# A 128-byte pad behind the bias table, and another start for the weights of the seven-product tiles: the phase in SBUF of matmul operands in a one-core decoder layer

## The chip, the core and the metric

One Trainium2 chip, of which the kernel uses one core. The metric is device time in microseconds, the median of three runs; lower is better. Matmuls run on TensorE (PE, with its weight loads listed as PEld), elementwise work on VectorE (DVE), ScalarE (ACT) and GpSimd (POOL); SyncE (SP) issues the transfers. SBUF is the on-chip memory: 128 partitions, and in each of them tiles lie one behind another. The *phase* of an operand is here its byte address within a partition, modulo 256.

## The reference

A decoder layer for 512 tokens of width 1024 in float32: a SwiGLU FFN of width 2816, a mixer of three parallel branches (sparse attention, gated delta rule, cross-attention into 256 memory tokens), and a second FFN.

```python
h = swiglu(rms_norm(x, ffn1_pre_norm[l]), ffn1_w_gate[l], ffn1_w_up[l], ffn1_w_down[l])
x = x + 0.5 * rms_norm(h, ffn1_post_norm[l])
u = rms_norm(x, mix_pre_norm[l])
nsa_q, nsa_kv, nsa_g, dn_qkv, dn_a, dn_b, dn_z, mem_q = split_cols(u @ w_in[l], IN_SPLITS)
...
gates = jax.nn.sigmoid(u @ w_branch_gate[l]).reshape(b, s, N_BRANCH, d)
merged = (gates[:, :, 0] * (o_nsa @ w_branch_nsa[l])
          + gates[:, :, 1] * (o_dn @ w_branch_dn[l])
          + gates[:, :, 2] * (o_mem @ w_branch_mem[l]))
x = x + rms_norm(merged @ w_out[l], mix_post_norm[l])
h = swiglu(rms_norm(x, ffn2_pre_norm[l]), ffn2_w_gate[l], ffn2_w_up[l], ffn2_w_down[l])
x = x + 0.5 * rms_norm(h, ffn2_post_norm[l])
```

## The kernel before

**Split products.** A float32 product is made of three products of rounded operands (type float32r): each operand is a high part, rounded, and a low part, the rest; `mm3` (lines 117 to 119) adds high by high, low by high and high by low in one PSUM bank. Weights come in pieces of 128x512 (256 KB): `wload` (line 105 the transfer into `wraw`, line 106 the rounding into `whi` on ScalarE, line 109 the rest `wlo` on VectorE). Tokens lie in `xth` and `xtl`, eight pieces of 128x512 each.

**Which operand is moving.** A matmul loads 128 columns of one operand (the stationary one) and streams the other (the moving one). In `prod_fm` the weights are stationary and `xth`/`xtl` move: gate and up products, projections, merge gates. In `tm_prod` and `down_half` the tokens or hidden parts (`Hh`, `Hl`) are stationary and the weights move; the down product of FFN 2 rounds most of its weights into a ring (`ringr`, `ringh`) that lies where `xth` and `xtl` did.

**Seven-product tiles.** From the seventh tile on, both FFNs make gate and up by a scheme of seven products in place of eight (`fast_load`, `fast_tile`): per tile 7 x 4 x 3 = 84 matmuls of 256 columns at line 429. The transformed tokens lie in `thi` and in low parts `txa`, `txb`, `tmth`, `tmtl`. The weights of even and odd tiles alternate between two sets: one in a tile `fset` (high, and behind it low parts), one in the room of `xth` and `xtl`, by then free (`fxth`, `fxtl`). `fast_set` lets a set begin `OFFW` floats behind the start of its room.

**Where things lie.** The pools stand one behind another. In the first one (`cp`) come the constants (4096 bytes per partition, from a multiple of 256 on), `xth`, `xtl` (16384 each), `RB` (1024), the room with the tag `mth` and that with the tag `mtl`. A room is as large as its largest tile. For `mth` this is the bias table's one-hot operand, 4 x 504 + 128 floats, 8576 bytes, which is 33.5 times 256; so `mtl` and every pool behind it begin at a phase of 128. In the built program the operands of the large groups have these phases:

| group (line) | moving | stationary |
|---|---|---|
| gate, up, projections: `xth`/`xtl` by `whi`/`wlo` (117 to 119) | 0 | 128 |
| `w_vs`, `w_z`: `whi`/`wlo` by `xth`/`xtl` | 128 | 0 |
| down product: `whi`/`wlo` by `Hh`/`Hl`; `w_out` | 128 | 128 |
| down product of FFN 2, ring: `ringh` (`wlo`) by `Hh`/`Hl` | 0 (128) | 128 |
| seven products, `fset`: `thi`, `txa`, `txb`, `tmtl` (`tmth`) | 128 (0) | 64 |
| seven products, `fxth`: the same | 128 (0) | 192 |
| attention logits `KH`/`KL` by `qa` (1039) | 128 | 128 |

**The start.** The first 256 tokens come in two halves of columns, the other 256 (`xb`) later. A list (`order_s` in `PRM`) says in which order pieces of work are written: `w` a weight load of the first two tiles, `P` half of their products, `t` a transposition of two column blocks with its rounding (lines 198 to 201), `x` the load of the later tokens, `n` their squares, inverse root and scaling (lines 184, 129 to 139, 187, 188), `R` the row scale `RB` of the first tokens (lines 229 to 238), `F` the gate of a tile for a half of the tokens (with its products, where `P` did not make them; lines 300 to 306), `B` the loads of the bias table, `c` those of the other constants. `offs` raises the priority of a piece by a number of places in the scheduler. Each engine takes its instructions strictly in the order so found, and SP its transfers.

Of the kernel before, what the change touches and what calls it, by code (L numbers as in the profile page):

```python
# [10 lines left out]
F32 = mybir.dt.float32  # L11
# [6 lines left out]
P = 128  # L18
# [7 lines left out]
NH = 8  # L26
# [4 lines left out]

C_ID, C_TRI, C_NEG, C_LVL, C_EYE, C_END = 0, 128, 256, 384, 768, 1024
M_BM, M_HB = 0, 8
PAD = 88


PRM = {'order': ['i', 'a', 'w', 'c01', 'h01', 'r0', 'c00', 'c10', 'c02', 'l0', 'h00', 'h02', 'c12', 'k0', 'h10', 'c11', 'c22', 'h12', 'h11', 'h22', 'r1', 'k1', 'l1', 'c21', 'h21', 'b0', 'e0', 'z', 'c20', 'r2', 'h20', 'c32', 'k2', 'l2', 'c31', 'd00', 'h31', 'r3', 'd01', 'l3', 'b1', 'd02', 'x0', 's00', 'e1', 'd10', 'c30', 'h32', 'x1', 'd11', 's01', 'h30', 's02', 's03', 'q3', 'p0', 'd12', 'o0', 'p1', 'q0', 'p2', 'p3', 'k3', 's10', 'p4', 'q1', 'p5', 's11', 'p6', 'p7', 's12', 's13', 'o1', 'q2', 'f'], 'dma': {'l': 'sync', 'b': 'sync', 'd': 'scalar', 'c': 'sync', 'r': 'sync'}, 'off': {'b0': 300, 'h31': 400, 'r1': 50, 'h32': 50, 'h11': 100, 'h12': 200, 'd10': 100, 'A01': 100, 'A10': 100, 'A11': 100, 'A20': 400, 'A31': 100, 'A21': 20, 'x0': 20, 'x1': 20, 'L': 200, 'S310': 400, 'S001': 20, 'S311': 400, 'A30': 100, 'r0': 400, 'd02': 20, 's11': 100, 'V20': 400, 'l3': 100, 'q1': 20, 'f': 400, 'l1': 50, 'h20': 100, 'h22': 100, 'r3': 50, 'P010': 50, 'y': 100, 'h02': 50, 'S101': 20, 'A00': 100, 'Q0': 50, 'Q1': 200, 'Q2': 50, 'Q3': 50, 'P110': 400, 'V31': 400, 'd01': 200, 'o0': 400, 'p0': 50, 'p1': 400, 'p2': 400, 'p4': 400, 'p5': 400, 'p6': 400, 'p7': 400, 'b1': 200, 'h01': 100, 'M15': 20, 'P201': 400, 'e0': 100, 'e1': 100, 'o1': 20, 'q0': 50, 'q2': 20, 'h21': 20, 'd11': 50, 'p3': 400, 'U0': 100, 's13': 50, 'c11': 20, 's00': 200, 'P011': 400, 'M14': 200, 'c20': 50, 'k2': 20, 'M03': 20, 'V00': 400, 'V01': 400, 'V10': 400, 'V11': 400, 'V21': 400, 'V30': 400, 'l2': 200, 'h00': 400, 'G0': 20, 'S210': 20, 'P101': 200, 'i': 100, 'G2': 20}, 'ph': 'e', 'po': 'ss', 'xpd': (0, 1, 2), 'order2': ['K1', 'K0', 'B', 'M10', 'Q0', 'C0', 'Q1', 'S000', 'S001', 'P000', 'C3', 'P001', 'C1', 'S010', 'P010', 'C2', 'S011', 'V00', 'Q2', 'S101', 'S100', 'P011', 'S110', 'V01', 'M12', 'P100', 'W0', 'P101', 'S111', 'Q3', 'P110', 'S200', 'S210', 'V10', 'P111', 'V11', 'P200', 'M14', 'M15', 'S201', 'P201', 'S211', 'W1', 'V20', 'P211', 'P210', 'V21', 'S301', 'W2', 'S300', 'S311', 'M11', 'P300', 'P301', 'L', 'M13', 'S310', 'G0', 'V30', 'M16', 'G2', 'P311', 'M17', 'P310', 'V31', 'W3', 'A00', 'M00', 'A01', 'G1', 'U0', 'M05', 'A10', 'A11', 'G3', 'A30', 'A31', 'U3', 'U1', 'M03', 'M06', 'A20', 'A21', 'U2', 'M07', 'M22', 'M20', 'M02', 'M24', 'M27', 'M21', 'M23', 'M01', 'M25', 'M04', 'M26'], 'order0': ['d0', 'p0', 'n0', 't0', 'd1', 'k2', 'k0', 'p2', 'p3', 'v', 'k3', 'n1', 'k1', 't1'], 'order3': ['s2', 's3', 's7', 's6', 's5', 's1', 's0', 's4', 'd00', 'd01', 'd11', 'g', 'p0', 'd10', 'n0', 't0', 'p1', 'n1'], 't3': (('mm', 'r'), ('e', 's')), 'pool': {'W2': 2, 's13': 3, 'k0': 0, 'k1': 0, 'k2': 0, 'k3': 2, 'p3': 1, 'C0': 1, 'C1': 0, 'C2': 0, 'C3': 2, 'S310': 0, 'L': 3, 'd11': 3, 'p0': 1, 'p1': 1, 'p2': 1, 'p4': 2, 'p5': 1, 'p6': 1, 'p7': 1, 'S311': 0, 'h01': 0, 'h00': 2, 'h02': 0, 'h10': 0, 'h11': 0, 'h12': 0, 'h22': 0, 'h21': 0, 'h20': 0, 'h31': 0, 'h30': 3, 'h32': 0, 'i': 2, 'P011': 2, 'c21': 0, 'd01': 2, 'S000': 0, 'S001': 0, 'S010': 0, 'S011': 0, 'S100': 0, 'S101': 0, 'S110': 0, 'S111': 0, 'S200': 0, 'S201': 0, 'S210': 0, 'S211': 0, 'S300': 0, 'S301': 0, 'M24': 2, 'G2': 2, 'A01': 0, 'M10': 0, 'M15': 2, 'M12': 2, 'M14': 2, 'M13': 2, 'M17': 2, 'M11': 2, 'M16': 2, 'M23': 0, 'M27': 3, 'M01': 2, 'M00': 2, 'M03': 0, 'M07': 2, 'M06': 1, 'M22': 2, 'M04': 2, 'M20': 2, 'M26': 2, 'M02': 0, 'M21': 2, 'M25': 2, 'M05': 2, 'c11': 1, 'o1': 3, 'P000': 2, 'P001': 1, 'P010': 2, 'P100': 2, 'P101': 2, 'P110': 2, 'P111': 2, 'P200': 2, 'P201': 2, 'P210': 2, 'P211': 2, 'P301': 0, 'P300': 3, 'P310': 2, 'P311': 2, 'c12': 3, 'b1': 1, 'x0': 0, 'x1': 0, 'V21': 0, 'c30': 0, 'c01': 0, 'c02': 0, 'c00': 0, 'c10': 0, 'c22': 0, 'c20': 0, 'c31': 0, 'c32': 0, 's01': 3, 'A31': 0, 'd12': 0, 'y': 2, 'G0': 2, 'G1': 2, 'G3': 0, 'U3': 0, 'W3': 2, 'r1': 2, 's12': 3, 'U2': 0, 'Q0': 2, 'Q1': 2, 'Q2': 2, 'Q3': 1, 's00': 3, 's02': 2, 's03': 3, 's10': 2, 's11': 3, 'e1': 2, 'd00': 1, 'U0': 0, 'U1': 0, 'l2': 0, 'd02': 2, 'K1': 3, 'V11': 0, 'V00': 2, 'r2': 0, 'l3': 3}, 'pool3': {'d00': 3, 'd01': 3, 'd10': 3, 'd11': 0, 'p1': 2, 't1': 3, 't0': 3, 's5': 2, 's7': 2, 's1': 2, 's0': 2, 's3': 2, 's6': 2, 's2': 2, 's4': 2, 'q0': 1}, 'pool0': {}, 'off0': {'p3': 20, 'n1': 50, 'k2': 400, 'k1': 20, 'p2': 100, 'p0': 400}, 'off3': {'s1': 20, 's5': 200, 'g': 200, 't0': 200, 'd10': 200, 'p0': 200, 'n0': 200}, 'tt': ('e', 's'), 'order_s': ['t00', 'w010', 'w000', 't01', 'P00', 'w110', 'y', 'w100', 'P10', 't02', 'w011', 'w001', 't03', 'P01', 'w111', 'w101', 'R0', 'F000', 'P11', 'x', 'n', 't10', 'F200', 't11', 'F101', 't12', 't13', 'F110', 'B', 'F211', 'F011', 'c'], 't0': ('e', 's'), 'rs': ((0, 0), (0, 0)), 'ra': (1, 1), 'warm': 8, 'pools': {'F000': 0, 'F101': 0, 'F200': 0, 'F011': 0, 'F110': 0, 'F211': 0, 'w10': 0, 'w11': 1, 't00': 0, 't01': 0, 't02': 0, 't03': 0, 't13': 0, 't10': 0, 't11': 0, 't12': 0, 'w00': 0, 'w01': 0, 'w000': 0, 'P01': 0}, 'ptc': 'vvs', 'cva': 'v', 'offs': {'t13': 100, 'R1': 400, 't03': 20, 't02': 20, 'w001': 100}, 'vnc': 's', 'sp3': 0, 'hsc': 'vv', 'sf2': 2, 'psc': 'vvvv', 'sp1': 0, 'vbs': 'v', 't1c': 'vs', 'sgv': 256}


class Body:  # L40
    def __init__(self, ctx, tc, a, out, tap):
        self.tc, self.nc, self.a, self.out, self.tap = tc, tc.nc, a, out, tap
        pool = lambda name, **k: ctx.enter_context(tc.tile_pool(name=name, **k))
# [267 lines left out]

    OFFW = 48
    T_B11, T_B21, T_B22, T_T1, T_T2, T_T3, T_T4 = range(7)
    S_A11, S_A12, S_A22, S_S3, S_S1, S_S4, S_S2 = range(7)

# [540 lines left out]
        nc = self.nc  # L858
        rb = self.sp.tile([33, NH], F32, name="rb", bufs=1)
        oh, rows = room  # L860
        rw = oh[:33, 4 * 504 :].rearrange("p (h r) -> p h r", h=NH)
        dt = self.dr.tile([NH, self.RR, RL], F32, name="dtb")
        dc = self.dr.tile([NH, 16 * NJ], F32, name="dtc")
        n = self.RR // 16
# [310 lines left out]
                "F": tile,  # L1175
            }
            with tc.tile_pool(name="wx0", bufs=1) as self.wx:
                dt, dc, load, part = self.bias_table([self.cp.tile([P, n], F32, tag=t, name="room") for t, n in (("mth", 4 * 504 + P), ("mtl", 4 * 504))])
                step, full = self.fast_tokens(xh, xl, RB, H[:, FT - 16 :])
                task["B"] = load  # L1180
                self.tasks(task, PRM["order_s"], key="s")
# [352 lines left out]
```

## Time and profile before

| | |
|---|---|
| median of three runs | 1344.37 us (1342.34 to 1346.0) |
| the profiled execution's own time | 1346.39 us |
| its span, first to last instruction | 1344.6 us |
| granted TensorE clock in it | 0.999 of full speed |
| PE, PEld busy | 98%, 84% of the span |
| DVE, ACT, POOL busy | 67%, 53%, 10% |
| DMA, mean over the span | 133 GB/s |

The prediction reads five views. The *page* gives busy times and the chain of work that ended last. The *groups* put together instructions of one line, engine and tile: busy time, mean nanoseconds of one, idle time just before them and who ended it. The *timeline* lists instructions in order of time: start and duration in microseconds, engine, line, operation, out<-in, shape and count; for a matmul the moving operand is named first. Its durations reach from a matmul's start to its last result, and neighbours overlap, so what a matmul costs in a dense stretch is the distance of two starts. The *windows* give, for a stretch, each engine's busy time and its instructions in brackets, then clock, DMA share and GB/s. The list of *DMA issues* gives the size of one transfer.

### The profile page before, as it was taken

Reading aid. Unit: us, or ns where it says so; the run is one execution under the profiler, and the core shown is the slowest. Engines: PE = TensorE matmul, PEld = TensorE weight load, DVE = VectorE, ACT = ScalarE, POOL = GpSimd, SP = SyncE. Lnnn points to the kernel's source line nnn. Section 1 sums busy time; section 2 is a strip of 40 time slices with the busy share of each in tenths; the row PEclk is TensorE's granted clock in tenths of the full one; section 3 lists DMA queues with packets and bytes.
Section 4 is the critical chain, followed back from the end, with each engine's and each line's share of the span. In section 5 each row is a group of like instructions: output and inputs, shape, how many; then the busy total and the mean of one; then the engine's idle time right before and its main releaser. Section 6 shows DMA issues by size and latency. Waiting matters only on the chain.

```text
span 1344.6 us, 21791 instructions
## 1 busy us (share of the span) xinstructions
PE 1316.8 (98%) x7839; PEld 1124.6 (84%) x7839; DVE 904.3 (67%) x1805; ACT 713.2 (53%) x1536; POOL 139.5 (10%) x126
## 2 busy tenths in 40 slices
PE   8999999999999899999999999999999999999997
PEld 7889999788887778787777877888788899998886
DVE  6897876778567866846887333322788778766765
ACT  7566664767456444316655334333585556646642
POOL 0020000000012222003110212333200000000000
PEclk9999999999999999999999999999999999999999
DMA  7643331577664341323121222533735433317673
GB/s 242 208 150 115 103 119 33 179 253 244 190 189 119 92 123 49 105 87 120 54 70 33 79 71 71 188 95 110 250 119 164 129 107 111 110 33 255 208 223 105
DMA packets 106301, 178.32 MB, mean 133 GB/s; under 512 B 18781, under 2 KB 28369, under 8 KB 106193
## 3 DMA queue, kind: packets, MB, share of 16 engines
q1 hardware_dynamic: 105904, 176.67, 41.9%
q8 instruction: 61, 1.00, 0.3%
q14 instruction: 48, 0.39, 0.1%
q10 hardware_dynamic: 288, 0.26, 0.1%
HBM read 166.84 MB, written 10.01 MB: 132 GB/s over the span
## 4 chain that ended last, share of the span: by engine, by line
PE 85%; DVE 6%; DMA 4%; ACT 2%; issue 2%; SPq 1%; POOL 0%; DVEq 0%; ACTq 0%
PE smm L429 10%; PE pfm L117 7%; PE pfm L118 7%; PE pfm L119 7%; PE se L429 7%; PE ss L429 3%; PE acc_s L119 2%; PE acc_s L117 2%; PE acc_s L118 2%; PE ps L1039 2%; PE sr L429 2%; PE so L429 1%; PE acc_e L118 1%; DVE wlo L109 1%; PE acc_e L119 1%
## 5 line engine op out<-in xcount | busy, mean ns | idle before, releaser
L106 ACT CAST whi<-wraw 128x512 fp32r<-128x512 f32 (+1 forms) x314 | 190.8, 615 | 177.7 <-PE pfm L119 65.1
L109 DVE TENSOR_TENSOR wlo<-wraw,whi 128x512 fp32r<-128x512 f32 (+1 forms) x271 | 188.7, 704 | 108.4 <-ACT whi L106 103.4
L117 PE MATMUL pfm<-xth,whi 128*128 128x512 f32 x384 | 156.1, 409 | 1.5 <-ACT whi L106 1.0
L118 PE MATMUL pfm<-xth,wlo 128*128 128x512 f32 x384 | 154.4, 404 | 0.6 <-DVE wlo L109 0.6
L119 PE MATMUL pfm<-xtl,whi 128*128 128x512 f32 x384 | 154.5, 404 | 0.0
L117 PEld LDWEIGHTS pfm<-xth,whi 128*128 128x128 f32 x384 | 72.3, 189 | 19.2 <-issue 2.8
L118 PEld LDWEIGHTS pfm<-xth,wlo 128*128 128x128 f32 x384 | 72.4, 189 | 15.6 <-DVE wlo L109 1.1
L119 PEld LDWEIGHTS pfm<-xtl,whi 128*128 128x128 f32 x384 | 72.4, 188 | 14.8 <-issue 0.2
L106 ACT CAST ringh<-ringr 128x512 fp32r<-128x512 f32 x82 | 50.0, 620 | 44.1 <-DMA ringr<-in_ffn_d_dram 11.0
L109 POOL TENSOR_TENSOR wlo<-wraw,whi 128x512 fp32r<-128x512 f32 (+1 forms) x40 | 49.9, 1247 | 191.2 <-ACT whi L106 178.4
L429 PE MATMUL smm<-thi,fset 128*128 128x256 f32 x384 | 69.4, 279 | 0.0
L109 DVE TENSOR_TENSOR wlo<-ringr,ringh 128x512 fp32r<-128x512 f32 x75 | 51.2, 690 | 18.7 <-PE acc_e L119 8.2
L429 PEld LDWEIGHTS smm<-thi,fset 128*128 128x128 f32 x384 | 58.5, 188 | 0.2
L445 DVE TENSOR_TENSOR up<-smm,s 128x256 f32<-128x256 f32 x32 | 13.6, 424 | 66.5 <-ACT se L442 66.5
L429 PE MATMUL smm<-thi,fxtl 128*128 128x256 f32 x192 | 53.5, 279 | 0.6 <-DVE fxtl L411 0.6
L429 PE MATMUL smm<-thi,fxth 128*128 128x256 f32 x192 | 53.3, 277 | 0.0
L429 PE MATMUL se<-thi,fset 128*128 128x256 f32 x256 | 46.7, 280 | 0.0
L1042 ACT ACTIVATE Pm<-Pm,nm 128x128 f32<-128x128 f32 (+1 forms) x64 | 35.6, 558 | 14.2 <-DVE nm L1041 13.8
L123 DVE TENSOR_TENSOR Hl<-H,Hh 128x256 fp32r<-128x256 f32 x88 | 35.0, 421 | 6.9 <-ACT Hh L122 5.7
L402 DVE TENSOR_TENSOR fs<-fq 128x1024 f32<-128x1024 f32 x32 | 39.0, 1220 | 0.8 <-DMA fq<-in_ffn_u_dram 0.8
L429 PEld LDWEIGHTS se<-thi,fset 128*128 128x128 f32 x256 | 39.1, 187 | 0.0
L429 PEld LDWEIGHTS smm<-thi,fxtl 128*128 128x128 f32 x192 | 36.1, 188 | 1.0 <-DVE fxtl L411 1.0
(565 smaller groups left out, 3918.0 us busy)
## 6 DMA issues: line engine op xcount, KB each, us to landing
wraw<-in_ffn_d_dram SPq DMA_DIRECT2D x94, 256.0 KB, 2.9
ringr<-in_ffn_d_dram SPq DMA_DIRECT2D x82, 256.0 KB, 3.0
fq<-in_ffn_g_dram SPq DMA_DIRECT2D x64, 256.0 KB, 2.8
fq<-in_ffn_u_dram SPq DMA_DIRECT2D x64, 256.0 KB, 3.1
wraw<-in_w_gate_dram SPq DMA_DIRECT2D x48, 256.0 KB, 2.7
wraw<-in_ffn_u_dram SPq DMA_DIRECT2D x34, 256.0 KB, 3.2
wraw<-in_ffn_g_dram SPq DMA_DIRECT2D x34, 256.0 KB, 3.3
woraw<-in_w_out_dram SPq DMA_DIRECT2D x32, 256.0 KB, 3.9
```

Source lines behind the costliest of these rows:

```text
L106: nc.scalar.copy(hi, raw)
L109: eng.tensor_tensor(lo, raw, hi.bitcast(F32), op=OP.subtract)
L117: t.matmul(out, lh, rh, start=first, stop=False)
L118: t.matmul(out, ll, rh, start=False, stop=False)
L119: t.matmul(out, lh, rl, start=False, stop=last)
L123: return self.nc.vector.tensor_tensor(lo, src, hi.bitcast(F32), op=OP.subtract)
L402: add = lambda *x: v.tensor_tensor(*x, op=OP.add)
L429: m = lambda x, y, **kw: te.matmul(out, x, y, skip_group_check=True, **kw)
L445: v.tensor_tensor(up[:, 256:], a, s7, op=OP.add)
L1039: te.matmul(s[:, : max(n, 256)], A[:, qb * P : qb * P + P], K[j][:, : max(n, 256)], start=j == 0, stop=j == 1)
L1042: nc.scalar.activation(pm, pm, AF.Exp, bias=nm[:, qb : qb + 1], scale=-1.0, accum_out=sm[:, qb : qb + 1])
```

## The change

```diff
...
-'order_s': ['t00', 'w010', 'w000', 't01', 'P00', 'w110', 'y', 'w100', 'P10', 't02', 'w011', 'w001', 't03', 'P01', 'w111', 'w101', 'R0', 'F000', 'P11', 'x', 'n', 't10', 'F200', 't11', 'F101', 't12', 't13', 'F110', 'B', 'F211', 'F011', 'c']
+'order_s': ['t00', 'w010', 'w000', 't01', 'P00', 'w110', 'w100', 'y', 'P10', 't02', 'w011', 'w001', 't03', 'P01', 'w111', 'w101', 'R0', 'F000', 'P11', 'x', 'F101', 'n', 'F200', 't10', 't11', 't12', 't13', 'c', 'F110', 'B', 'F211', 'F011']
...
-'offs': {'t13': 100, 'R1': 400, 't03': 20, 't02': 20, 'w001': 100}
+'offs': {'t13': 100, 'R1': 400, 't03': 20}
...
-    OFFW = 48
+    OFFW = 16
...
-        rw = oh[:33, 4 * 504 :].rearrange("p (h r) -> p h r", h=NH)
+        rw = oh[:33, 4 * 504 : 4 * 504 + P].rearrange("p (h r) -> p h r", h=NH)
...
-                dt, dc, load, part = self.bias_table([self.cp.tile([P, n], F32, tag=t, name="room") for t, n in (("mth", 4 * 504 + P), ("mtl", 4 * 504))])
+                dt, dc, load, part = self.bias_table([self.cp.tile([P, n], F32, tag=t, name="room") for t, n in (("mth", 4 * 504 + P + 32), ("mtl", 4 * 504))])
```

Two entries of a further table (`pools`, for `w000` and `P01`) go as well; they held its default.

The pad of 32 floats makes the room `mth` 8704 bytes, 34 times 256. All tiles behind it lie 128 bytes further on. `OFFW` is 64 bytes in place of 192. In the built program every row of the table above then has moving phase 0, and stationary phase 0, or 64 for both sets of the seven-product tiles.

The list `order_s` moves instructions in the first 50 us; from there on PE, DVE, ACT, POOL and SP have the same order as before.

On SP, in the loads of the start, the second half of the tokens (`xb`, line 510) stands behind the weights of the third tile, and the constants (`cst`, line 1164) follow it (one piece of the difference):

```order
+L105 DMA wraw<-in_ffn_u_dram 128x512 x2
+L510 DMA xb<-in_x_dram 128x1024 x2
+L1164 DMA cst<-in_consts_dram 128x896
+L1165 DMA msk<-in_masks_dram 128x9
+L105 DMA wraw<-in_ffn_g_dram 128x512 x2
+L105 DMA wraw<-in_ffn_u_dram 128x512 x2
 L873 DMA rb<-in_rel_bias_dram 32x8
-L510 DMA xb<-in_x_dram 128x1024 x2
-L105 DMA wraw<-in_ffn_u_dram 128x512 x2
-L105 DMA wraw<-in_ffn_g_dram 128x512 x2
-L105 DMA wraw<-in_ffn_u_dram 128x512 x2
```

`xb` and its two transfers now come after two more loads of 256 KB; the constants come before eight weight loads that they followed.

On VectorE, the end of the inverse root for `xb` (lines 134 to 139) up to its scaling (line 187), before:

```order
L134 TENSOR_TENSOR rnz<-rnz,rnm 128x2
L135 SCALAR_TENSOR_TENSOR rnz<-rnz 128x2
L305 TENSOR_TENSOR sg<-sg,RB 128x256
L136 SCALAR_TENSOR_TENSOR rny<-rnz,rny 128x2
L306 TENSOR_TENSOR H<-sg,pu 128x256
L137 TENSOR_TENSOR rnz<-rny 128x2
L109 TENSOR_TENSOR wlo<-wraw,whi 128x512
L138 SCALAR_TENSOR_TENSOR rnz<-rnz,rnm 128x2
L109 TENSOR_TENSOR wlo<-wraw,whi 128x512
L139 SCALAR_TENSOR_TENSOR rny<-rnz,rny 128x2
L300 TENSOR_TENSOR sg<-pg,RB 128x256
L187 TENSOR_SCALAR xb<-xb,rny 128x512 x2
```

and with the change:

```order
L109 TENSOR_TENSOR wlo<-wraw,whi 128x512
L135 SCALAR_TENSOR_TENSOR rnz<-rnz 128x2
L300 TENSOR_TENSOR sg<-pg,RB 128x256
L136 SCALAR_TENSOR_TENSOR rny<-rnz,rny 128x2
L109 TENSOR_TENSOR wlo<-wraw,whi 128x512
L137 TENSOR_TENSOR rnz<-rny 128x2
L305 TENSOR_TENSOR sg<-sg,RB 128x256
L138 SCALAR_TENSOR_TENSOR rnz<-rnz,rnm 128x2
L109 TENSOR_TENSOR wlo<-wraw,whi 128x512
L139 SCALAR_TENSOR_TENSOR rny<-rnz,rny 128x2
L109 TENSOR_TENSOR wlo<-wraw,whi 128x512
L187 TENSOR_SCALAR xb<-xb,rny 128x512 x2
```

Between the start of the inverse root (line 129) and line 187 there are now five splits (line 109) in place of three, and eight gate steps (lines 300, 305, 306) in place of four.

On PE, the third and fourth transposition of the first tokens (`ptr<-cst,xa`, four column blocks), which stood between products, now stand in one block. Before:

```order
L117 MATMUL pu<-xth,whi 128x256
L198 MATMUL ptr<-cst,xa 128x128
L118 MATMUL pu<-xth,wlo 128x256
L198 MATMUL ptr<-cst,xa 128x128
L119 MATMUL pu<-xtl,whi 128x256
L117 MATMUL pu<-xth,whi 128x256
L198 MATMUL ptr<-cst,xa 128x128
```

With the change:

```order
L119 MATMUL pg<-xtl,whi 128x256
L198 MATMUL ptr<-cst,xa 128x128 x8
L117 MATMUL pu<-xth,whi 128x256
L118 MATMUL pu<-xth,wlo 128x256
L117 MATMUL pg<-xth,whi 128x256
L118 MATMUL pg<-xth,wlo 128x256
```

The products behind the block read what the block makes, so nothing of PE's own stands between.

2 lines of the change are left out of this document (1 added, 1 removed).

## The prediction

> **What bounds the kernel now.** The page first: who is busy, then the chain of work that ended last.
>
> ```profile
> span 1344.6 us, 21791 instructions
> PE 1316.8 (98%) x7839; PEld 1124.6 (84%) x7839; DVE 904.3 (67%) x1805; ACT 713.2 (53%) x1536; POOL 139.5 (10%) x126
> ...
> PE 85%; DVE 6%; DMA 4%; ACT 2%; issue 2%; SPq 1%; POOL 0%; DVEq 0%; ACTq 0%
> ```
>
> TensorE holds 85% of the chain, so the kernel costs about what its matmuls cost from start to start. The "mean ns" of the groups does not show that: a 128x512 product has 409 ns there, latency included, while matmuls overlap. What counts is the **pitch**, the distance between starts, and the timeline has it. First two neighbouring fast tiles of FFN 1 (each 84 matmuls of 256 columns, line 429): tile A with weights in `fset` from 125.17, tile B with weights in `fxth`/`fxtl` from 135.00, the next A from 144.63.
>
> ```profile
> 125.17 0.39 PE L429 MATMUL smm<-thi,fset 128*128 128x256 f32 x2
> ...
> 130.76 0.40 PE L429 MATMUL smm<-thi,fset 128*128 128x256 f32 x2
> ...
> 135.00 0.28 PE L429 MATMUL smm<-thi,fxth 128*128 128x256 f32 x1
> ...
> 140.55 0.28 PE L429 MATMUL smm<-thi,fxth 128*128 128x256 f32 x1
> ...
> 144.63 0.39 PE L429 MATMUL smm<-thi,fset 128*128 128x256 f32 x2
> ...
> 145.99 0.39 PE L429 MATMUL so<-thi,fset 128*128 128x256 f32 x2
> ```
>
> A takes 9.83 us, B 9.63, for the same shapes, with no wait named in either. The last 36 matmuls of A (130.76 to 135.00) have a pitch of 117.8 ns, the same 36 of B (140.55 to 144.63) 113.3, and the first 12 of the next A (144.63 to 145.99) still 113.3. Only the places of the operands differ. In the built program `thi` lies 128 bytes into a step of 256, A's weights 64, B's 192. I write d for the stationary operand's phase less the moving one's, modulo 256: d is 192 in A, 64 in B. In the second and third product the low tokens (`tmth`) lie at phase 0, so the moving phase changes within the product; after that A stays at 118, while B returns to 113.3.
>
> The same for 512 columns: `se<-xth,whi` (moving phase 0, stationary 128, d = 128) and the down product of FFN 1 (both 128, d = 0).
>
> ```profile
> 63.93 0.40 PE L117 MATMUL se<-xth,whi 128*128 128x512 f32 x1
> ...
> 68.81 0.39 PE L117 MATMUL ss<-xth,whi 128*128 128x512 f32 x1
> ...
> 276.22 0.39 PE L117 MATMUL acc_mm<-whi,Hh 128*128 128x512 f32 x1
> ...
> 290.50 0.39 PE L117 MATMUL acc_o<-whi,Hh 128*128 128x512 f32 x1
> ```
>
> From 63.93 to 68.81 are 21 starts, a pitch of 232.4 ns; from 276.22 to 290.50 are 63, a pitch of 226.7. So at d = 0 and 64 matmuls run at a floor (226.7 for 512 columns, and exactly half of it, 113.3, for 256), at d = 128 and mostly at 192 some 4 to 6 ns above it.
>
> The Trainium skill, page "TensorE: Matmul & The Clock Gate", section "Step-by-step: what each phase is for", speaks against this change: PE has two independent SBUF read ports, and loading the next weights takes nothing from the running matmul's reads. By that rule the phases would not matter and the sum would be nothing; the two tiles above do not agree with it.
>
> **The change part by part.** The pad makes the room 8704 bytes instead of 8576, so all that lies behind it moves from phase 128 to 0: low tokens, weights, hidden parts, `thi`. `xth`, `xtl`, `ringh` stay at 0. With `OFFW` 16 both sets begin at 64. Every split product is then at d = 0, every fast tile at d = 64 with one moving phase throughout. No instruction is added or made longer. What each part of the program gives, against the profiled execution:
>
> *Fast tiles.* A pair costs 9.83 + 9.63 = 19.46 us; 168 x 113.3 ns is 19.04. There are 16 pairs (16 tiles in each FFN): **-6.7 us**. VectorE is the next engine; its busy 86.24 of 120 us says that it follows.
>
> ```profile
> 120.00:240.00 120.00, 120.00 (x1039) 120.00 (x1038) 86.24 (x103) 66.99 (x138) 0.00 (x0) 1.00 0.27 85
> ```
>
> *Products of the first FFN tiles on `xth`/`xtl`.*
>
> ```profile
> L117 PE MATMUL se<-xth,whi 128*128 128x512 f32 x32 | 12.8, 398 | 0.0
> ...
> L117 PE MATMUL pg<-xth,whi 128*128 128x256 f32 (+1 forms) x104 | 32.7, 315 | 1.3 <-ACT whi L106 0.6 <-ACT xth L200 0.4 <-DVE sg L300 0.3
> ...
> 36.04 0.28 PE L117 MATMUL pu<-xth,whi 128*128 128x256 f32 x1
> ...
> 46.72 0.28 PE L117 MATMUL pu<-xth,whi 128*128 128x256 f32 x1
> ```
>
> Six groups like the first (two banks, three lines) make 192 matmuls of 512 columns; of the six like the second, by the program 24 of each 104 are 512 wide, 144 in all: 336 x 5.7 ns = **-1.9 us**. The other 80 of each are 256 wide, 480 in all: 90 starts in 10.68 us, 118.7 ns. At 113.3 they save 2.6 us. A long run of 256 columns at d = 0 is not in the trace; between 0 and 2.6 I take **-2.0**, near the upper end, since 512 columns at d = 0 have exactly twice 113.3.
>
> *Merge stage.* 455 matmuls in 105 us, no idle time; about 12.6 tiles of 36, of which 24 read `xth`/`xtl` and some of the other 12 lie at d = 128 too: 330 x 5.7 = **-1.9 us**.
>
> ```profile
> 840.00:945.00 105.00, 105.00 (x455) 85.09 (x454) 33.51 (x48) 36.08 (x63) 35.78 (x26) 1.00 0.43 140
> ```
>
> *Down product of FFN 2 through the ring* (`ringh` at 0, `wlo` and `Hh` at 128: two of three matmuls at d = 128).
>
> ```profile
> L106 ACT CAST ringh<-ringr 128x512 fp32r<-128x512 f32 x82 | 50.0, 620 | 44.1 <-DMA ringr<-in_ffn_d_dram 11.0
> ...
> 1284.18 0.39 PE L117 MATMUL acc_e<-ringh,Hh 128*128 128x512 f32 x1
> ...
> 1286.93 0.39 PE L117 MATMUL acc_e<-ringh,Hh 128*128 128x512 f32 x1
> ```
>
> 12 starts in 2.75 us, 229.2 ns; 82 loads of 6 matmuls, each 2.5 ns less: **-1.2 us**.
>
> *Delta and attention stages.* The group `pfm<-xth,whi` has 384 matmuls, with L118 and L119 1152; less the merge stage's 300 some 850 are left, at 5.7 ns 4.8 us.
>
> ```profile
> L117 PE MATMUL pfm<-xth,whi 128*128 128x512 f32 x384 | 156.1, 409 | 1.5 <-ACT whi L106 1.0
> ...
> 380.00:560.00 180.00, 172.12 (x967) 143.82 (x965) 130.83 (x338) 85.46 (x196) 34.61 (x38) 1.00 0.36 104
> 560.00:840.00 280.00, 277.61 (x1517) 213.17 (x1517) 163.81 (x470) 127.41 (x340) 51.41 (x42) 1.00 0.25 77
> ```
>
> Here products stand between softmax and delta-rule pieces that wait for other engines: PE is idle for 7.9 us of the first window even by its own latency-stretched busy time. Some of the gain becomes waiting, and after each break matmuls need a while to fall into step (below). Bounds 0 and 4.8; I take half, **-2.4**.
>
> ```profile
> 262.28 0.40 PE L118 MATMUL acc_mm<-whi,Hl 128*128 128x512 f32 x1
> ...
> 263.20 0.39 PE L119 MATMUL acc_mm<-wlo,Hh 128*128 128x512 f32 x1
> ```
>
> These two, four starts apart just behind a transposition, give 230 ns though d = 0: the floor is reached only in runs.
>
> *The start's new order.* SP now sends two more weight loads ahead of the second half of x (`xb`), and the constants right behind it.
>
> ```profile
> wraw<-in_ffn_u_dram SPq DMA_DIRECT2D x34, 256.0 KB, 3.2
> ...
> 14.60 0.88 SPq L510 DMA_DIRECT2D xb<-in_x_dram  x2
> ...
> 19.39 1.06 ACT L184 ACTIVATE H<-xb 128x1024 bf16<-128x1024 f32 x1 [0.80 <-DMA xb<-in_x_dram]
> ...
> 25.32 0.69 DVE L109 TENSOR_TENSOR wlo<-wraw,whi 128x512 fp32r<-128x512 f32 x1
> ...
> 26.05 0.43 DVE L300 TENSOR_TENSOR sg<-pg,RB 128x256 f32<-128x256 f32 x1
> 26.39 0.87 DVE L187 TENSOR_SCALAR xb<-xb,rny 128x512 f32<-128x512 f32 x2
> ...
> 0.00:33.00 33.00, 29.46 (x204) 25.20 (x204) 22.44 (x61) 24.13 (x51) 1.24 (x8) 1.00 0.76 247
> 33.00:60.00 27.00, 27.00 (x176) 23.82 (x176) 22.13 (x32) 13.08 (x27) 0.92 (x1) 1.00 0.58 189
> ```
>
> ScalarE waits for `xb` at 19.39. Two loads more are 0.5 MB, 2.1 us at 247 GB/s, less what they gain by being issued sooner. Queued behind the squares of `xb` is, on ScalarE, the copy of `RB` (line 238), and on VectorE the gate products that free `pg` for the next tile and the scaling of `xb` (line 187), before whose end PE cannot transpose; ahead of it VectorE now has two more splits (0.69) and four more gate steps (0.43), 3.1 us. So the new order can lose some 5 us. Until 33 us PE has 3.5 us idle, its first wait for data included, and none from there to 60: it can win 3.5 at most. I take **+1.0**, about the middle. The eight transpositions of `xa`, now in one block, are the same eight; the first activation behind them is inside these bounds.
>
> Sum: -6.7 - 1.9 - 2.0 - 1.9 - 1.2 - 2.4 + 1.0 = -15.1 us. The profiled execution took 1346.39 us (span 1344.6 and 1.8 around it), which gives 1331.3; it lay 2.0 above the median of 1344.37, so **1329**.
>
> **The rivals.**
>
> *No effect*: 1344 us. The difference of A and B would come from something that stays, such as the banks or the order of the tiles. Against it stands that d = 0 and 128 part 512 columns in the same way in another stage, under other lines. The Trainium skill's rule, cited above, would give the same.
>
> *Half an effect*: only the fast tiles gain, since there one moving phase replaces two and the weights move by a measured d; products on `xth` and the ring keep their pitch, because something else about them (the 16 KB tile, three operands) is slow. -6.7 and +1.0: 1338.7, or 1339.
>
> *Slower, by the moving phase itself.* Every matmul of the trace at the floor has its moving operand at phase 128, and none with moving phase 0 is in it: `xth` (0) has 232.4, the ring 229.2. `tmth` with `fset`, moving 0 and stationary 64, is the very pair that all fast tiles get, and runs at 117 to 118 in tile A. If phase 0 of the moving operand is the slow one, whatever the weights do, then B falls to A's 9.83 (16 x 0.2 = 3.2 us) and about 1000 products at d = 0 (FFN 1's down product, `w_out`, attention's `KH`/`KL`, some merges) go from 226.7 to 232, 5.4 us: +8.6 and +1.0, 1354 us. It decides at the first B tile: 9.83 instead of 9.52. Against it stand two products with moving phase 128 that are slow: `thi` in A, and the token-major one.
>
> ```profile
> 491.41 0.39 PE L118 MATMUL ptm<-whi,xtl 128*128 128x512 f32 x1
> ...
> 492.81 0.39 PE L118 MATMUL ptm<-whi,xtl 128*128 128x512 f32 x1
> ```
>
> Six starts in 1.40 us are 233 ns with `whi` moving at 128 and `xth`/`xtl` stationary at 0, d = 128. And `tmth` stands in A among neighbours at d = 192, so its own pitch says little.
>
> *A stalled start*: +5 instead of +1, 1333 us, inside the range: VectorE's longer queue and the late `xb` are both felt in full.
>
> **How the numbers follow.** Forecast 0.70, half an effect 0.12, no effect 0.09, slower 0.06, a stalled start 0.03. A difference under 0.3% (4 us) cannot be told from none by a measurement of this kernel. Forecast, stalled start and nearly all of half an effect (0.11) lie beyond it: faster 0.84; no effect and the rest of the half 0.10; slower 0.06. The range goes down to 1320: the open terms at their better ends add 0.6 and 2.4, the start (-3.5 instead of +1.0) 4.5, in all 1321.5, and 1.5 more for the taken ones. Up to 1340: half an effect and a little. Outside are the two cases without a gain, 0.15, and some misses at the edges.
>
> **What would show it.** A and B tiles both 9.52 us; some 1060 matmuls in the window 120 to 240 in place of 1039; 21 starts of `se`/`ss` in 4.76 us; the merge stage 2 us shorter; the weight loads of PE, VectorE and ScalarE durations as before. The start right: the block of eight transpositions of `xb`, PE's wait for line 187, no more than some 1 us later than before. It would be wrong if B or the down product of FFN 1 grew, or if the split products kept 232 at d = 0.

## The result, and the profile after

| | median of runs | ratio, 95% interval | profiled execution, span |
|---|---|---|---|
| before | 1346.0 us (1342.34 to 1347.25, 7 runs) | | 1346.39, 1344.6 us |
| changed | 1336.48 us (1334.7 to 1340.93, 7 runs) | 0.9938 (0.9924 to 0.9952) | 1334.7, 1332.9 us |

That is 9.5 us between the medians, and 11.7 between the two profiled executions. The forecast was 15.1 less. The experiments below change what this result is worth: the same program, measured again, had 1346.04 us and was not faster than the kernel before at all.

The page of the changed kernel: as many matmuls, PE 14.9 us less busy, the chain much as before.

```profile
span 1332.9 us, 21794 instructions
...
PE 1301.9 (98%) x7839; PEld 1118.2 (84%) x7839; DVE 903.5 (68%) x1805; ACT 715.5 (54%) x1536; POOL 139.2 (10%) x126
...
PE 85%; DVE 6%; DMA 3%; ACT 3%; issue 2%; POOL 0%; SPq 0%; DVEq 0%; ACTq 0%
```

The timeline of PE in the same kernel: the first and last of 22 products on `xth`, 21 starts apart, then the starts of a tile A, a tile B and the next A.

```profile
77.92 0.39 PE L117 MATMUL se<-xth,whi 128*128 128x512 f32 x1
...
82.68 0.39 PE L117 MATMUL se<-xth,whi 128*128 128x512 f32 x1
...
127.57 0.39 PE L429 MATMUL smm<-thi,fset 128*128 128x256 f32 x2
...
137.09 0.28 PE L429 MATMUL smm<-thi,fxth 128*128 128x256 f32 x1
...
146.61 0.39 PE L429 MATMUL smm<-thi,fset 128*128 128x256 f32 x2
```

21 starts in 4.76 us (before 4.88), and both tiles 9.52 us (before 9.83 and 9.63): here it is as forecast. The first FFN's products of 256 columns do not meet it:

```profile
43.33 0.28 PE L117 MATMUL pu<-xth,whi 128*128 128x256 f32 x1
...
45.85 0.28 PE L117 MATMUL pu<-xth,whi 128*128 128x256 f32 x1
```

21 starts in 2.52 us are 120.0 ns, where before had 118.7 and the forecast 113.3.

The windows of the changed kernel (busy time of each engine, instructions in brackets), by stage: start, FFN 1's fast tiles, the two mixer stages, merge, FFN 2's fast tiles.

```profile
0.00:33.00 33.00, 26.39 (x178) 22.24 (x178) 20.05 (x55) 21.11 (x42) 0.89 (x8) 1.00 0.77 247
...
120.00:240.00 120.00, 120.00 (x1062) 120.00 (x1061) 88.98 (x106) 69.12 (x142) 0.00 (x0) 1.00 0.29 89
380.00:560.00 180.00, 172.55 (x982) 145.15 (x982) 131.30 (x347) 87.13 (x208) 34.58 (x38) 1.00 0.37 105
560.00:840.00 280.00, 276.54 (x1514) 213.27 (x1511) 162.37 (x460) 126.01 (x328) 52.74 (x43) 1.00 0.26 79
840.00:945.00 105.00, 105.00 (x464) 86.70 (x464) 35.40 (x51) 38.73 (x68) 35.75 (x26) 1.00 0.45 149
1080.00:1200.00 120.00, 120.00 (x1062) 120.00 (x1061) 91.84 (x108) 70.21 (x143) 0.00 (x0) 1.00 0.28 89
```

Merge has 464 matmuls in place of 455 in its 105 us, 2.0 us at 226.7 ns. The start lost: 178 matmuls in 33 us in place of 204. The timeline shows where the end of it comes from: scaling of `xb` (L187, before at 26.39), then the first transposition of `xb`, behind the last product that PE had.

```profile
30.44 0.28 PE L119 MATMUL pu<-xtl,whi 128*128 128x256 f32 x1
...
31.24 0.87 DVE L187 TENSOR_SCALAR xb<-xb,rny 128x512 f32<-128x512 f32 x2
...
31.82 0.41 PE L198 MATMUL ptr<-cst,xb 128*128 128x128 f32 x2 [1.10 <-issue]
```

PE stands idle there for more than 1 us. The row gives `issue`, so the profile names no waiter; that it is the scaling is read from the order of the rows. PE also stands idle for 1.00 us behind the block of eight transpositions, where before it had another product to do:

```profile
16.25 0.39 PE L117 MATMUL pu<-xth,whi 128*128 128x256 f32 x1 [1.00 <-ACT xth L200]
```

### The profile page after: what moved, and what is told of

The parts are those of the page before. It is cut to its first block, busy times and chain, and to the rows that moved or that the text cites. A ratio compares the mean times of both kernels' runs of the same rounds, so it can differ in the third digit from the quotient of the medians.

```text
span 1332.9 us, 21794 instructions
## 1 busy us (share of the span) xinstructions
PE 1301.9 (98%) x7839; PEld 1118.2 (84%) x7839; DVE 903.5 (68%) x1805; ACT 715.5 (54%) x1536; POOL 139.2 (10%) x126
## 4 chain that ended last, share of the span: by engine, by line
PE 85%; DVE 6%; DMA 3%; ACT 3%; issue 2%; POOL 0%; SPq 0%; DVEq 0%; ACTq 0%
PE smm L429 10%; PE pfm L117 7%; PE pfm L119 7%; PE pfm L118 7%; PE se L429 7%; PE ss L429 3%; PE acc_s L119 2%; PE acc_s L117 2%; PE acc_s L118 2%; PE ps L1039 2%; DVE wlo L109 2%; PE sr L429 2%; PE acc_mm L117 1%; PE so L429 1%; PE acc_mm L119 1%
## 5 line engine op out<-in xcount | busy, mean ns | idle before, releaser
L119 PEld LDWEIGHTS pfm<-xtl,whi 128*128 128x128 f32 x384 | 72.3, 188 | 13.7 <-issue 0.2
```

The costliest lines, as they stand in the source:

```text
L119: t.matmul(out, lh, rl, start=False, stop=last)
```

## The experiments

All but the two benches, which compute nothing of the layer, were timed against the kernel before, each group beside it on one chip: `places_only` to `w64` on one, the two `lo192` on another. There the kernel before had medians of 1344.42 to 1345.11 us. On which chip the first measurement was taken is not known. The counts are matmuls in 120 us of fast tiles, of one profiled execution each: at 113.3 ns 1059 fit in, at 117.7 some 1020. In `lo192` and `kick` the stage ends before 240 us, so their first count is lower.

| | median (range) | ratio, 95% interval | 120 to 240 | 1080 to 1200 |
|---|---|---|---|---|
| before | | | 1039 | 1038 |
| changed, first measurement | 1336.48 (1334.7 to 1340.93) | 0.9938 (0.9924 to 0.9952) | 1062 | 1062 |
| places_only | 1342.66 (1340.67 to 1344.49) | 0.9984 (0.9975 to 0.9993) | 1021 | 1022 |
| order_only | 1347.33 (1346.15 to 1348.65) | 1.0024 (1.0015 to 1.0032) | 1038 | 1038 |
| sets_zero | 1352.46 (1350.01 to 1353.37) | 1.0055 (1.0042 to 1.0068) | 1003 | 1002 |
| all_128 | 1346.6 (1345.15 to 1349.38) | 1.0017 (1.0008 to 1.0026) | 1022 | 1021 |
| kick | 1343.12 (1337.91 to 1344.1) | 0.9990 (0.9981 to 0.9999) | 1040 | 1022 |
| after_again | 1346.04 (1344.42 to 1349.02) | 1.0008 (0.9999 to 1.0017) | 1021 | 1022 |
| sets_192 | 1346.66 (1344.89 to 1348.26) | 1.0012 (1.0003 to 1.0021) | 1021 | 1021 |
| w64 | 1353.39 (1350.61 to 1354.31) | 1.0055 (1.0042 to 1.0068) | 1061 | 1021 |
| lo192 | 1331.46 (1328.17 to 1334.17) | 0.9896 (0.9879 to 0.9913) | 1045 | 1061 |
| lo192_after | 1335.64 (1333.99 to 1335.99) | 0.9925 (0.9912 to 0.9937) | 1061 | 1061 |

### First: the change taken apart

*places_only*: the changed kernel with the table `PRM` of before.

> The pad and the offset of the changed kernel, with the order of the start as it was before. Theory 1 (the places give 14.5 us, the new order takes some 3 back): 14.5 us less than before, about 1331 us, some 3 to 5 us less than the changed kernel; PE's idle time up to 60 us as before (9.9 us), one stretch of eight transpositions less. Rival (the order costs nothing, the places give only what the two medians differ by): 1336.5 us, like the changed kernel.

1342.66 us: neither. The products of 512 columns had gained all they were to gain (227.6 ns in the mean of neighbouring starts, as in the changed kernel, where before had 230.4), but the fast tiles ran at 117.7 ns, all but part of FFN 1's first two tiles, at the very phases that gave 113.3 in the changed kernel.

*order_only*: the kernel before with the table `PRM` of the change.

> The new order of the start alone, all operands where they were before. Theory 1: some 3 us slower than before, about 1349 us, with 12.9 us of PE idle up to 60 us in place of 9.9; tiles A and B 9.83 and 9.63 us as before. Rival (the order costs nothing): 1346 us. The forecast's own term: +1.0, 1347 us.

2.9 us slower than before: the order costs about what the trace of the result suggested (26 matmuls less in 33 us, some 3 us), and more than the forecast's 1.0. A single trace does not size it: this run's profiled execution has 1346.15 us, no more than that of before, and in two traces of the changed kernel the first fast matmul starts at 72.53 and at 70.79 us. Two more pairs differ in the order alone: `after_again` less `places_only` 3.4 us, `lo192_after` less `lo192` 4.2.

*sets_zero*: weights of the fast tiles at d = 0.

```diff
-    OFFW = 16
+    OFFW = 0
```

> The changed kernel with OFFW 0: weights of the fast tiles at phase 0, so 2688 matmuls of 256 columns at d = 0 in place of 64. Theory 1 (256 columns at d = 0 have a pitch of 119.8 ns, as in the changed kernel's first FFN tiles): A and B tiles 84 x 119.8 ns = 10.06 us, 2688 x 6.4 ns = 17 us more than the changed kernel, about 1353 us. Rival (d = 0 is at the floor for 256 columns as for 512, and the first tiles are slow for another reason, such as two banks in turn or the transfers of the start): tiles 9.52 us and 1336.5 us.

1352.46, theory 1. The windows of this kernel have 1003 and 1002 matmuls, about 120 ns each:

```profile
120.00:240.00 120.00, 120.00 (x1003) 120.00 (x1002) 88.93 (x105) 68.16 (x137) 0.00 (x0) 1.00 0.28 89
```

So d = 0, the best phase for 512 columns, is the worst of those used here for 256.

*all_128*: the changed kernel, all tiles 128 bytes further on.

```diff
-        self.cst = self.cp.tile([P, C_END], F32, name="cst")
+        self.cp.tile([P, 32], F32, name="pad"); self.cst = self.cp.tile([P, C_END], F32, name="cst")
```

> The changed kernel with 128 bytes put ahead of all its tiles: every moving operand at phase 128 in place of 0, every stationary at 128 or 192, all differences d as in the changed kernel. Theory 1 (only the difference d counts): 1336.5 us within 1 us, A and B tiles 9.52 us. Rival (the moving phase itself counts: 0 is the fast one, 128 the slow one): at least the tiles of 9.83 us again, 32 x 0.31 = 10 us more than the changed kernel, 1346 us or above.

1346.6 us, which looked like the rival's win. But the products of 512 columns kept the floor with the moving operand at 128 (227.6 ns in the mean again), and the tiles at 117.7 ns are those of `places_only`, where it is at 0. The moving phase was not what the two had in common.

### Second: one phase, two rhythms

Those two runs, `places_only` and `all_128`, asked for another theory (theory 3 in the expectations): at d = 64 with one moving phase, matmuls of 256 columns have two rhythms that keep themselves up, 113.3 and 117.7 ns (the expectations call them states).

*after_again*: the changed kernel, nothing else.

> The changed kernel itself once more. Theory 3 (two states, picked by chance): its times fall into groups some 5 us apart, by whether the fast tiles of one FFN, of both or of none run at 117.6 ns: 1334 to 1336, about 1340, or about 1346 us; a profile with a slow time shows whole FFN stages at 117.6. Rival (one state, and the first profile shows it): all executions within 1334 to 1338 us, and the tiles at 113.4 ns again.

1346.04 us, 11 runs from 1344.42 to 1349.02, none within 3 us of the first measurement's highest. The groups 5 us apart that theory 3 expected did not show: these eleven lie within 4.6 us, and six of the first measurement's seven within 3.3 (the seventh, 1340.93, may be one with a slow FFN). So the rhythm is hardly drawn anew in each execution. The windows of its two fast stages:

```profile
120.00:240.00 120.00, 120.00 (x1021) 120.00 (x1020) 87.35 (x103) 67.33 (x139) 0.00 (x0) 1.00 0.27 87
1080.00:1200.00 120.00, 120.00 (x1022) 120.00 (x1021) 92.92 (x109) 71.04 (x144) 0.00 (x0) 1.00 0.30 95
```

The same program has 41 and 40 matmuls less than at the first measurement. FFN 2 is slow from its first tile on; FFN 1 began at 113.3, too. The timeline shows the place where the two part, the first tile B, at the product that takes bank `smm` over from ScalarE's copy (line 438). In the first measurement the copy starts at 103.91, takes 0.37, and PE has:

```profile
104.31 0.28 PE L429 MATMUL se<-txa,fxth 128*128 128x256 f32 x1
104.42 0.29 PE L429 MATMUL smm<-thi,fxth 128*128 128x256 f32 x1
104.55 0.28 PE L429 MATMUL smm<-thi,fxtl 128*128 128x256 f32 x1
104.67 0.28 PE L429 MATMUL smm<-txb,fxth 128*128 128x256 f32 x1
104.79 0.28 PE L429 MATMUL smm<-thi,fxth 128*128 128x256 f32 x1
104.90 0.28 PE L429 MATMUL smm<-thi,fxtl 128*128 128x256 f32 x1
105.01 0.28 PE L429 MATMUL smm<-txb,fxth 128*128 128x256 f32 x1
```

and in the second:

```profile
102.57 0.28 PE L429 MATMUL se<-txa,fxth 128*128 128x256 f32 x1
102.69 0.29 PE L429 MATMUL smm<-thi,fxth 128*128 128x256 f32 x1
102.81 0.28 PE L429 MATMUL smm<-thi,fxtl 128*128 128x256 f32 x1
102.93 0.28 PE L429 MATMUL smm<-txb,fxth 128*128 128x256 f32 x1
103.05 0.28 PE L429 MATMUL smm<-thi,fxth 128*128 128x256 f32 x1
103.17 0.28 PE L429 MATMUL smm<-thi,fxtl 128*128 128x256 f32 x1
```

The first is held up by some 27 ns (104.31 to 104.79 is 0.48, four starts at 113.3 are 0.45) and is then back at 113 (104.79, 104.90, 105.01). The second is held up by some 15 ns (102.57 to 102.81), goes on at 118 (102.93, 103.05, 103.17) and stays there for the 1200 matmuls to the end of the stage. Five more stages with this d come to the same place at 113.3. Where the delay is one distance of 124 to 129 ns, the slow rhythm follows (also FFN 1 of `places_only`, FFN 2 of `all_128` and of `w64`); where it is one of 133 ns, or two long ones close together, the quick one goes on (also FFN 2 of the first measurement, FFN 1 of `w64`). These are seven cases, not an experiment. No row names the wait; that it is one for the copy is read from the order of the rows and was not tried by itself.

*kick*: `places_only` with `tmth` 128 bytes further on, so that two of seven products change the moving phase.

```diff
-        lo = [p.tile([P, 2, 4, 256], F32R, tag=t, name="t" + t, bufs=1) for p, t in ((self.tp, "xa"), (self.tp, "xb"), (self.cp, "mth"), (self.cp, "mtl"))]
+        lo = [p.tile([P, o + 2048], F32R, tag=t, name="t" + t, bufs=1)[:, o:].rearrange("p (a b t) -> p a b t", a=2, b=4) for p, t, o in ((self.tp, "xa", 0), (self.tp, "xb", 0), (self.cp, "mth", 32), (self.cp, "mtl", 0))]
```

> places_only with one edit: the tile tmth of the fast tiles lies 128 bytes further on, so that two of the seven products have a moving operand that goes from phase 0 to 128 and back (d 64, 64, 192). Theory 3 (256 columns at d = 64 with one moving phase have two states that last, 113.3 and 117.6 ns, and a small disturbance picks one; a change of moving phase inside a product brings them back to 113.3, as in the B tiles of before): all fast tiles 9.52 to 9.6 us, 2688 x 4.2 ns = 11 us less than places_only, about 1331.5 us. Rival (the change of phase cures nothing, or disturbs by itself): tiles of 9.8 us or more, 1342 us or above, like places_only.

1343.12 us, as the rival has it. In the profiled execution it worked by half: in FFN 1 every tile but the first ones fell to 117.7 in the products with `tmth` and returned to 113.3 behind them; in FFN 2 none returned (1022 matmuls). But that execution, at 1337.91, is the fastest by 4.3 us. The other ten have 1342.25 to 1344.1, like `places_only`, so most likely hardly any tile returned there; no trace shows them. A change of phase is no sure cure.

*sets_192*: the changed kernel with `OFFW` 48.

> The changed kernel with OFFW 48: weights of the fast tiles at 192 with one moving phase 0. If d = 192 is like 64, a state that lasts (113.3 or 117.6) is picked by chance and the time is between 1336 and 1347 us. If d = 192 falls to the slow state by itself, as tiles A of before suggest, all tiles take 9.83 to 9.88 us and the time is 1346 us. If d = 192 is slower still, as d = 0 is with 119.95 ns, above 1350 us.

1346.66 us and 1021 matmuls in both windows: the second of the three cases. At d = 192 with one moving phase the slow rhythm is the one that lasts.

*w64*: all split weights (`whi`, `wlo`) 64 bytes further on, by small pads ahead of and behind their pool, and ahead of the start's extra one.

```diff
-        self.wp = pool("wp", bufs=1)
+        pool("pa", bufs=1).tile([P, 16], F32, name="pa"); self.wp = pool("wp", bufs=1); pool("pb", bufs=1).tile([P, 48], F32, name="pb")
...
+                self.wx.tile([P, 16], F32, name="px"); ...
```

> The changed kernel with the split weights whi, wlo 64 bytes further on and all else as it was: the first FFN tiles' 480 products of 256 columns at d = 64 in place of 0, the split products of 512 columns at d = 64 (1752) or, token-major and down products, at 192 (804). Theory 1: the first FFN tiles lose 6.4 ns each, 3 us less; if 512 columns at d = 64 are at the floor too, 1333 us in all, and if they have 232 ns there, 1752 x 5.4 ns = 9.5 us come on top, 1343 us. Rival (the first FFN tiles are slow for other reasons than d): their pitch stays at 119.8.

1353.39. Between 33 and 60 us the first FFN's 256 columns now run at 113.7 ns, so their 120 was the phase and nothing else of that stage. The 512 columns at d = 64 take 233.3 in the mean. In the profiled execution FFN 2's fast tiles were in the slow rhythm (1021), some 5 us more, and FFN 1's in the quick one (1061): one execution has both.

### Third: phases by themselves

*bench*: no other engine works; the three matmuls of a fast tile's step, again and again, at 16 phases.

```python
t(b[:, :n], m(w, i, d), mh, ...)        # wh, th
t(b[:, :n], m(w, i + 28, d), mh, ...)   # wl, th
t(b[:, :n], m(w, i, d), ml, ...)        # wh, tl
```

> A kernel of its own that computes nothing of the reference (its output is a constant): dense products of 256 columns as in a fast tile (wh, wl, wh against th, th, tl), no other engine at work, moving phase 0, stationary phase 0 to 240 in 16 steps of 16 bytes (tiles pa to pp), 11 stretches of 36 matmuls for each, parted by one odd matmul (other width, or a moving phase of 128); then 512 columns in 8 steps of 32 bytes (qa to qo), 6 stretches of 24. Theory 3: at d = 64 (pe) some stretches run at 113.3 ns and some at 117.6, by what came before, d = 0 (pa) at 120, d = 192 (pm) at 117.8; for 512 columns d = 0 (qa) all at 226.7, d = 128 (qi) at 229 to 238. Rival (the two states need the traffic of the other engines or of the DMA queues): each phase has one pitch here, and pe is 113.3 in all 11 stretches. Open: whether some phase gives 113.3 in all 11 stretches with 256 columns; that one would be the place for the weights.

The timeline of `pe` (d = 64), line 1532, one matmul in three: the first stretch, the odd matmul (line 1540), the second stretch.

```profile
204.45 0.28 PE L1532 MATMUL pe<-th,w 128*128 128x256 f32 x1
...
207.85 0.28 PE L1532 MATMUL pe<-th,w 128*128 128x256 f32 x1
208.19 0.28 PE L1540 MATMUL pe<-tl,w 128*128 128x256 f32 x1
...
208.65 0.28 PE L1532 MATMUL pe<-th,w 128*128 128x256 f32 x1
...
212.19 0.28 PE L1532 MATMUL pe<-th,w 128*128 128x256 f32 x1
```

30 starts in 3.40 us, 113.3 ns, and 30 in 3.54, 118: same operands, same phases, nothing else at work. The mean pitch of each stretch (its last fifteen or so starts, in ns; the first stretch of `pa` is left out):

```text
256 columns  d =   0   120.0 in all
             d =  64   113.3 117.8 117.7 113.3 117.7 117.8 117.8 113.3 113.3 117.7 113.3
             d = 128   118.7, once 120.0
             d = 192   117.7 to 117.8 in all
             others    116.5 to 120.2, two stretches of 122.9
512 columns  d =   0   226.7 in all
             d = 192   228.9 in all
             others    231.9 to 234.3
```

Theory 3 holds without any traffic: d = 64 has both rhythms, the other phases named have the pitch expected. No step of 16 bytes gives 113.3 always.

*bench2*: the low weights and the low tokens moved apart from the high ones, 64 pairs; and odd matmuls of a fixed width.

> A second kernel of its own, again without anything of the reference: 256 columns, wh at phase 64 and th at 0 throughout; the low weights wl at 0 to 224 in steps of 32 (first letter a to h behind the c) and the low tokens tl at 0 to 224 (second letter), 4 stretches of 30 matmuls for each pair, parted by a matmul of 146, 200 or 236 columns; then all three at d = 64, with 5 times the same odd matmul of 64 to 254 columns between stretches of 24 (waw to wpw). Theory 3: cca (wl 64, tl 0: the changed kernel) has both 113.3 and 117.7; a few pairs may hold 113.3 in all four stretches, as the B tiles of before do, since a change of phase inside the triple moves a matmul against its weight load; an odd matmul of a given width always leads to the same state, whichever came before. Rival (113.3 needs d = 64 in all three, and the state behind a disturbance is chance): no pair but cca ever shows 113.3, and the same width leads now to the one state and now to the other.

```text
cca (wl 64, tl 0, as changed)   117.8 113.3 113.3 113.3
cga (wl 192, tl 0)              113.3 113.3 113.3 113.3
the other 62 pairs              116.6 to 122.2, never 113.3

odd matmul of 128 columns       113.3 117.8 113.3 117.8 113.3 117.8
              136               117.8 113.3 117.8 113.3 117.8 113.3
              192, 208, 224     113.3 in all six
              248               117.8 in all six
```

The first figure of a row stands ahead of the odd matmuls, the others behind one each. One pair ended every stretch at 113.3. Four stretches alone would say little, since `cca` is at 113.3 behind the same three odd matmuls. But the trace has `cga` slow first and then quick, within one stretch (rows of line 1533, one matmul in three):

```profile
711.99 0.28 PE L1533 MATMUL cga<-th,w 128*128 128x256 f32 x1
...
712.69 0.28 PE L1533 MATMUL cga<-th,w 128*128 128x256 f32 x1
...
713.03 0.28 PE L1533 MATMUL cga<-th,w 128*128 128x256 f32 x1
...
714.05 0.28 PE L1533 MATMUL cga<-th,w 128*128 128x256 f32 x1
```

Six starts in 0.70 us are 117 ns, then nine in 1.02 us 113.3, with nothing between that disturbs. So it goes in three of its four stretches, while the slow stretch of `cca` stays at 118 for all of its 30 matmuls. That is a rhythm that comes back by itself.

That a width always leads to the same rhythm holds for 192, 208, 224 and 248, and for 112 (five times 113.3); but with most widths the pattern repeats every stretch, every second or (96 columns: 117.8 113.3 117.8, twice) every third, so that here it is hardly chance.

### Fourth: the pair in the kernel

*lo192* (order of before) and *lo192_after* (order of the change): the low weights of both sets begin 128 bytes behind the high ones' phase.

```diff
-        return [x[:, o : o + n].rearrange("p (q c) -> p q c", q=7) for x in (h, l)]
+        return [x[:, p : p + n].rearrange("p (q c) -> p q c", q=7) for x, p in ((h, o), (l, o + 32))]
```

> places_only with one edit: the low parts of the fast tiles' weights begin 128 bytes further on (phase 192), the high parts stay at 64, the pair that held 113.3 ns in all its stretches (cga). Theory 3: every fast tile 9.52 us in both FFNs, whatever disturbs them; 32 tiles x 0.36 us = 11.5 us less than places_only, about 1331.5 us, and no groups of times 5 us apart. Rival (the pair was lucky in four stretches, or the traffic of the kernel upsets it): tiles at 9.8 us or a mixture, 1337 to 1343 us.

> The same edit on the changed kernel with its new order of the start. Theory 3: all fast tiles 9.52 us, the time of the changed kernel with both FFNs at 113.3, 1334 to 1336 us in every execution, some 3 us above lo192 by the new order. Rival: as the changed kernel once more, 1344 to 1349 us.

1331.46 and 1335.64, both as theory 3 has it. The timeline of `lo192` at the same disturbance:

```profile
99.47 0.28 PE L429 MATMUL se<-txa,fxth 128*128 128x256 f32 x1
99.58 0.29 PE L429 MATMUL smm<-thi,fxth 128*128 128x256 f32 x1
99.71 0.28 PE L429 MATMUL smm<-thi,fxtl 128*128 128x256 f32 x1
99.83 0.28 PE L429 MATMUL smm<-txb,fxth 128*128 128x256 f32 x1
99.94 0.28 PE L429 MATMUL smm<-thi,fxth 128*128 128x256 f32 x1
100.06 0.28 PE L429 MATMUL smm<-thi,fxtl 128*128 128x256 f32 x1
100.17 0.28 PE L429 MATMUL smm<-txb,fxth 128*128 128x256 f32 x1
```

Held up once more (99.58 to 99.71 is 0.13), it goes on at 113, as the first measurement of the changed kernel did. `lo192_after` shows more at this place:

```profile
103.97 0.28 PE L429 MATMUL smm<-thi,fxth 128*128 128x256 f32 x1
...
104.68 0.28 PE L429 MATMUL smm<-thi,fxth 128*128 128x256 f32 x1
...
104.91 0.28 PE L429 MATMUL smm<-txb,fxth 128*128 128x256 f32 x1
...
105.93 0.28 PE L429 MATMUL ss<-tmtl,fxth 128*128 128x256 f32 x1
```

Six starts in 0.71 us are 118 ns, then nine in 1.02 us 113.3: it runs at the slow distance for six matmuls and comes back, as `cga` does in the bench. FFN 2 of `lo192` has

```profile
1080.00:1200.00 120.00, 120.00 (x1061) 120.00 (x1061) 88.96 (x106) 69.20 (x142) 0.00 (x0) 1.00 0.29 90
```

`lo192` has 13.7 us less than before. Against the changed kernel, `lo192_after` is the fair comparison, since it has the same order of the start: 0.8 us less than its first measurement, 10.4 less than its second. Neither `places_only` nor the changed kernel was timed on the chip of the `lo192` runs, so the times alone do not show that the pair makes the difference; that the quick rhythm comes back by itself is what the two traces above show.

## Why the prediction was right or wrong

Step by step, with what the traces of before and of the result give when what exceeds 113.3 or 226.7 ns is added up over the neighbouring starts of a stage:

| step | forecast, us | measured, us |
|---|---|---|
| fast tiles | -6.7 | -6.6 in the first measurement; +4.6 in `after_again` |
| 512 columns on `xth`/`xtl` | -1.9 | -1.9 |
| first FFN, 256 columns | -2.0 | +0.4 |
| merge | -1.9 | -2.1 |
| FFN 2's ring | -1.2 | -1.1 |
| delta and attention | -2.4 | -3.3 of pitch, +0.8 of waits |
| new order of the start | +1.0 | +2.9, +3.4, +4.2 in three pairs |

With -6.6 for the fast tiles and 3.5 for the order the right column adds up to -10.3, between the medians' -9.5 and the profiled pair's -11.7. With +4.6 it is +0.9; `after_again` measured +1.5 against its own before. Without the order and with -6.6 it is -13.8; `lo192` measured -13.7. Of the forecast's -15.1, then, the first measurement lacked 4.8 us, and two terms account for it: 2.4 by the 256 columns at d = 0, 2.5 by the start.

**The mechanism was right in part.** The phases of the two operands bear on the pitch of PE, and for 512 columns d alone set it: 226.7 ns at 0, some 232 at 128. For 256 columns d was not enough. The Trainium skill, page "TensorE: Matmul & The Clock Gate", section "Step-by-step: what each phase is for", has the weight load take nothing from the running matmul's reads. By that rule, as the prediction worked it out, the phases would not matter; the benches, with no other engine at work, go from 113.3 to 122 ns by phases alone and do not agree with that. Whether it is the weight load that disturbs the reads was not tried. The rival *no effect* gives `after_again`'s time, but its reason falls. *Slower by the moving phase itself* falls as well: 512 columns at d = 0 have the same floor with the moving operand at 0 and, in `all_128`, at 128.

**"Every fast tile at d = 64 with one moving phase throughout"** is the step that failed worst. It took 113.3 for a property of d. It is one of two rhythms, and with one moving phase nothing in the tile brings the quick one back: in `after_again` the same tiles have 117.7, and the term is +4.6 in place of -6.7. That the first measurement has -6.6 is luck. The trace of before had two hints, and the prediction quoted both. A's first 12 matmuls are "still 113.3", though at d = 192, so a pitch could outlast the phase that it came from. And B "returns to 113.3" behind the products with `tmth`. That was read as the merit of d = 64; the change of moving phase that the edit took away may have been what reset it. In the profiled execution of `kick` such a change resets FFN 1's tiles and not FFN 2's.

**The 256 columns at d = 0** were taken near the better end of their bounds, since 512 columns at d = 0 had twice 113.3. The inference from one width to the other was wrong: 120.0 ns, +0.4 in place of -2.0, the other end and a little beyond.

**The start** was mis-sized: +1.0 from bounds of -3.5 to +5, where three pairs say 3 to 4. The mechanisms named are those in the trace (the late scaling of `xb`, PE idle for 1.1 us before its transposition, and the wait behind the block of eight, which the prediction had put inside its bounds); what was counted on against them, that PE had 3.5 us to win, did not come.

Open is what in the chip makes the rhythms, and why the first measurement's profile stays quick behind its disturbances while the second's does not. The delays there differ, some 27 ns against 15, but what sets their length was not tried. Nor was it tried whether the chip or the occasion decides: both rhythms were seen in each bench, and in one execution of `w64`, so neither belongs to one chip alone; but the two measurements of the changed kernel may differ in the chip, and which rhythm a kernel falls into may depend on it.

## What to carry to other kernels

When matmuls stream without a break, look at the distance of their starts, not at their durations, and compare it between operands that differ only in place. A pitch that a trace shows is not a constant of the layout: before building on it, see whether the same operands ever show another one, and measure a change of layout on more than one occasion. A small bench over phases, with small disturbances thrown in, found here a placement that recovers by itself; look for that recovery inside a stretch, since a stretch that merely stays quick may be quick by luck.

## What the runs showed of the hardware

- Matmuls of 256 float32r columns whose weights begin at a phase 64 bytes above the moving operand's (modulo 256) run at 113.3 or at 117.7 ns, for over a thousand matmuls on end (first measurement, `after_again`). Behind one distance of 124 to 129 ns four stages switched to 117.7; behind longer delays three went on at 113.3.
- Behind an odd matmul of 128 columns the rhythm alternated each time; behind 112, 192, 208 or 224 it was 113.3, behind 248 117.8 (`bench2`, five times each).
- With the low weights at 192, the high ones at 64 and the moving operands at 0 the quick rhythm came back by itself, within some ten matmuls, behind every disturbance seen (`bench2`, `lo192`, `lo192_after`).
- d = 0 is the floor for 512 columns (226.7 ns) and among the slowest for 256 (120.0); the other phases tried cost 512 columns 2 to 8 ns (`bench`).
